# Attention output evacuated per two head pairs, and PSUM banks handed out in the order of their release

## The chip, the core and the metric

The kernel runs on one core of one Trainium2 chip. The metric is device time in microseconds of one execution, and the time before is the median of three runs. The engines are called as in the profile: PE is TensorE (matmuls; PEld is its loading of weights), ACT is ScalarE, DVE is VectorE, POOL is GpSimd, and SP issues nearly all of the DMAs. The granted clock of TensorE is given as a share of its full speed.

## What is computed

A trunk of two layers over 256 tokens of width 1024. Each layer is a SwiGLU feed-forward, a token mixer, and a second feed-forward, all with RMS norms before and after and with residual sums. The mixer of the first layer is a gated linear recurrence; that of the second is a causal attention with 16 heads of width 64 and a forget bias, whose keys and values come from the stream after the first layer. All weights are float32 and are read from HBM. The change touches the attention:

```python
def forgetting_attention(xq, w_q, w_o, k, v, c):
    Bn, S, _ = xq.shape
    q = (xq @ w_q).reshape(Bn, S, N_HEADS, HEAD_DIM).transpose(0, 2, 1, 3) * (HEAD_DIM ** -0.5)
    outs = []
    for blk in range(S // Q_BLOCK):
        q0 = blk * Q_BLOCK
        end = q0 + Q_BLOCK
        logits = jnp.einsum('bhqd,bhkd->bhqk', q[:, :, q0:end], k[:, :, :end]).astype(jnp.float32)
        logits = logits + c[:, :, q0:end, None] - c[:, :, None, :end]
        ...
        p = jax.nn.softmax(logits, axis=-1).astype(v.dtype)
        outs.append(jnp.einsum('bhqk,bhkd->bhqd', p, v[:, :, :end]))
    o = jnp.concatenate(outs, axis=2).transpose(0, 2, 1, 3).reshape(Bn, S, D_ATTN)
    return o @ w_o
```

## The kernel before

**Tiling.** The 256 tokens are two tiles of 128, t = 0 and t = 1. Every float32 product is made of three: a weight is split into an upper half `whi` (ACT, L200) and a lower half `wlo` (DVE, L201), and so are the activations; `mm3` (L208 to L210) multiplies x-upper by whi, x-upper by wlo, and x-lower by whi into one PSUM bank. Weights arrive in 512 KB pieces; there are nine buffers for split weights, so a split of a later piece waits until TensorE has done with the piece that held its buffer.

**Banks.** PSUM is one tile `pall` of eight banks. `bank(kind)` hands them out from three lists: "mm" (0 to 3, for accumulators and small transposes), "gt" (4, 5) and "tr" (6, 7). It takes the first bank of the list that is neither held nor lent, and puts it at the list's end; with `hold` the bank stays taken until `release`. With `again` it takes the last free one of the list in place of the first. `release` only ends the hold, so the list is in the order of handing out. The waits that guard a bank are made by the framework from who reads and writes it.

**Attention.** `attention(t)` makes a list of steps. A step holds up to three pieces for different score groups: `values(i - 3)`, `turn(i - 2)` and `logits(i)`. A group is two head pairs for t = 0 (four groups) and one pair for t = 1 (eight groups).
- `logits` multiplies queries with keys (L1155) into two of the banks 4 to 7; DVE adds the bias (L1162) and takes the maximum (L1164), ACT makes the exponentials `pe` (L1170), DVE the reciprocal of their sum (L1172) and the product (L1173).
- `turn` transposes `pe` on TensorE (L1179) into an "mm" bank, taken with `again`; ACT copies it to `pT` (L1181).
- `values` multiplies `pT` with the values (L1193) into the held "mm" bank `po`. A bank holds four head pairs. When it is full, ACT copies it to `oh` (L1199), DVE subtracts to get `ol` (L1200), and the bank is released.

The queries are made by the projection before it (`heads_T`, whose ACT copy to `qT` is L1025), and the output projection (`row_items`, `mm3` on `oh` and `ol`) takes one head pair k = 0 to 7 as a row; the last two rows of a tile are kept and done together. `enter` then norms the sum and adds it to `h` (L315, L319).

**Order.** TensorE's order is written by hand. In the attention it is the string `ATT_ORDER`: "0" and "1" are the next unit of the query or output projection for that token tile, "a0" and "a1" the next step of the attention of that tile. So the projection rows of t = 0 run between the attention steps of t = 1. The framework's scheduler sets the order on ACT and DVE, which work in order, each instruction waiting for its inputs, its buffer and its bank.

Of the kernel before, what the change touches and what calls it, by code (L numbers as in the profile page):

```python
# [9 lines left out]
F32 = mybir.dt.float32  # L10
F32R = mybir.dt.float32r
BF16 = mybir.dt.bfloat16
AF = mybir.ActivationFunctionType
ALU = mybir.AluOpType
AX = mybir.AxisListType

P = 128
D = 1024
S = 256
# [26 lines left out]
def trunk_kernel(ctx: ExitStack, tc: tile.TileContext, A: dict, out: bass.AP):  # L46
    nc = tc.nc
# [11 lines left out]
    def nm(s):  # L59
        uid[0] += 1  # L60
        return f"{s}_{uid[0]}"

    pall = psum.tile([P, 8, 512], F32, name="pall")
    lent = set()
    order = {"mm": [0, 1, 2, 3], "gt": [4, 5], "tr": [6, 7]}
    held = {}

    def bank(kind, hold=False, again=False):

        free = [i for i in order[kind] if i not in held and i not in lent]  # L70
        i = free[-1 if again else 0]
        order[kind].remove(i)
        order[kind].append(i)
        b = pall[:, i, :]
        if hold:
            held[i] = b
        return b

    def release(*banks):
        for b in banks:  # L80
            for i in [i for i, v in held.items() if v is b]:
                del held[i]

    def mmbank():
        return bank("mm", True)

    def gtbank():
        return bank("gt")

    def trbank(hold=False):  # L90
        return bank("tr", hold)
# [326 lines left out]
    def proj_items(w, c0, nn, get_x, post, nk=8):  # L418

        kper = min(1024 // nn, 4)  # L420
        acc = {}

        for k0 in range(0, nk, kper):
            kn = min(kper, nk - k0)

            def prep(k0=k0, kn=kn):
                return split(load_raw(w[k0 * P:(k0 + kn) * P, c0:c0 + nn].rearrange("(k p) n -> p k n", p=P), P, kn * nn),
                             P, kn * nn)

            def work(t, u, k0=k0, kn=kn):  # L430
                if k0 == 0:
                    acc[t] = mmbank()
                ps = acc[t][:, :nn]
                for j in range(kn):
                    k = k0 + j
                    mm3(ps, *get_x(t, k), u.hi[:, j * nn:(j + 1) * nn], u.lo[:, j * nn:(j + 1) * nn], k == 0, k == nk - 1)
                if k0 + kn == nk:
                    post(t, acc[t][:, :nn])
                    release(acc[t])
            items.append((prep, work))  # L440
# [23 lines left out]
    def row_items(w, widths, get_x, post, rows=2):  # L464


        acc = {}
        kept = [[], []]
        nk = len(widths)
        r0 = 0  # L470
        for k, kp in enumerate(widths):
            def prep(kp=kp, r0=r0):
                return split(load_raw(w[r0:r0 + kp, :], kp, D), kp, D)

            def work(t, u, k=k):
                if k == 0:
                    acc[t] = [mmbank(), mmbank()]
                m = rows if t == 1 else min(rows, 2)
                if k >= nk - m:
                    kept[t].append((k, u))  # L480
                    if k < nk - 1:
                        return
                    todo = [(kk, uu, n) for n in range(2) for (kk, uu) in kept[t]]
                else:
                    todo = [(k, u, n) for n in range(2)]
                for (kk, uu, n) in todo:
                    mm3(acc[t][n], *get_x(t, kk), uu.hi[:, n * 512:(n + 1) * 512], uu.lo[:, n * 512:(n + 1) * 512],
                        kk == 0, kk == nk - 1)
                if k == nk - 1:
                    post(t, acc[t])  # L490
                    release(*acc[t])
            items.append((prep, work))
            r0 += kp
# [624 lines left out]
    att = {}  # L1118
# [17 lines left out]
    def attention(t):  # L1136

        ap = pools["a"]
        nk = t + 1
        per = 4 // nk  # L1140
        np_ = per // 2
        w = nk * P
        box = {}
        G = NH // per

        def head(hg, b, j):
            return 2 * (hg * np_ + j) + b

        def logits(hg):
            c = 4 + (hg % 2) * 2  # L1150
            lg = pall[:, c:c + 2, :S]
            for j in range(np_):
                for b in range(2):
                    p = hg * np_ + j
                    nc.tensor.matmul(lg[:, b, j * w:(j + 1) * w], att["q"][t][b * HD:(b + 1) * HD, p, :],  # L1155
                                     kv["kT"][b * HD:(b + 1) * HD, p, :w], start=True, stop=True)
            v = lg.rearrange("p b (j k) -> p j b k", j=np_)
            h0 = hg * per
            bias = att["nb"][t][:, h0:h0 + per, :].rearrange("p (j b) k -> p j b k", b=2)
            if np_ == 1:  # L1160
                v, bias = lg, att["nb"][t][:, h0:h0 + per, :]
            nc.vector.tensor_tensor(v, v, bias, ALU.add)  # L1162
            mx = spool.tile([P, 4], F32, tag="mx", name=nm("mx"))[:, :per]
            nc.vector.tensor_reduce(mx, lg.rearrange("p b (j k) -> p b j k", j=np_), AX.X, ALU.max, negate=True)  # L1164
            sm = spool.tile([P, 4], F32, tag="sm", name=nm("sm"))[:, :per]
            pe = box["pe", hg] = ap.tile([P, per, w], F32, tag="pe", name=nm("pe"), bufs=2)
            for b in range(2):
                for j in range(np_):
                    i = b * np_ + j
                    nc.scalar.activation(pe[:, i, :], lg[:, b, j * w:(j + 1) * w], AF.Exp, bias=mx[:, i:i + 1],  # L1170
                                         accum_out=sm[:, i:i + 1])
            nc.vector.reciprocal(sm, sm)  # L1172
            nc.vector.tensor_tensor(pe, pe, sm.unsqueeze(2).to_broadcast([P, per, w]), ALU.mult)  # L1173

        def turn(hg):
            tp = bank("mm", again=True)
            pev = box["pe", hg].rearrange("p a b -> p (a b)")
            for j in range(4):
                nc.tensor.transpose(tp[:, j * P:(j + 1) * P], pev[:, j * P:(j + 1) * P], ident)  # L1179
            pT = box["pT", hg] = ap.tile([P, 4, P], F32, tag="pT", name=nm("pT"), bufs=2)  # L1180
            nc.scalar.activation(pT.rearrange("p a b -> p (a b)"), tp, AF.Copy)  # L1181

        def values(hg):
            p0 = hg * np_
            if p0 % 4 == 0:
                box["po"] = mmbank()
            po, pT = box["po"], box["pT", hg]
            for j in range(np_):
                o = (p0 + j) % 4 * P
                for k in range(nk):  # L1190
                    for b in range(2):
                        hd = head(hg, b, j)
                        nc.tensor.matmul(po[b * HD:(b + 1) * HD, o:o + P], kv["v"][k][:, hd * HD:(hd + 1) * HD],  # L1193
                                         pT[:, (b * np_ + j) * nk + k, :], start=k == 0, stop=k == nk - 1)
            if (p0 + np_) % 4 == 0:
                b = (p0 + np_) // 4 - 1
                oh_v = att["oh"][t][:, 4 * b:4 * b + 4, :].rearrange("p a b -> p (a b)")
                ol_v = att["ol"][t][:, 4 * b:4 * b + 4, :].rearrange("p a b -> p (a b)")
                nc.scalar.activation(oh_v, po, AF.Copy)  # L1199
                nc.vector.tensor_tensor(ol_v, po, oh_v.bitcast(F32), ALU.subtract)  # L1200
                release(po)

        steps = []
        for i in range(G + 3):
            s = []
            if 0 <= i - 3 < G:
                s.append(lambda i=i: values(i - 3))
            if 0 <= i - 2 < G:
                s.append(lambda i=i: turn(i - 2))
            if i < G:  # L1210
                s.append(lambda i=i: logits(i))
            steps.append(s)
        return steps
# [13 lines left out]
    ffn_d = ffn_items(lambda: pools["f"], A["ffn2_w_gate"][1], A["ffn2_w_up"][1], A["ffn2_w_down"][1], A["ffn2_post_g"][1],  # L1227
                      lambda t, hid: None, last=True)

    ATT_ORDER = ("0 0 0 0 0 0 0 a0 0 a0 1 1 1 a0 1 1 a0 1 1 a0 1 a1 0 a0 0 a1 0 a0 0 a1 0 a1 0 a1 0 a1 0 a1 1 a1 1 a1 1 a1 1 a1 1 1 1 1")  # L1230


    def half(t, i):
# [139 lines left out]
    nxt = [n_ffn3, n_ffn3]  # L1373
    for c in ATT_ORDER.split():
        if c[0] == "a":
# [45 lines left out]
```

## Time and profile before

| | us |
|---|---|
| median of three runs (lowest, highest) | 1004.15 (1004.14, 1004.41) |
| the profiled execution | 1002.69 |
| its span, from first to last instruction | 1001.0 |
| mean granted clock of TensorE | 0.997 |
| attention and output projection, from the span's start | about 738 to 812 |

The profile is of one execution. A row of the timeline has the start and the length in us, the engine, the line of the kernel, the operation, what it writes and reads, how many instructions were merged, and in brackets the engine's idle time before it with what ended that. A row of a stretch has its length, each engine's busy time with its number of instructions, the granted clock, the DMA share and GB/s. Where a line was used for several shapes, a group's mean mixes them.

### The profile page before, as it was taken

To read this page: it belongs to the slowest core of one execution; us is meant where nothing else is said; L and a number is where in the kernel's file an instruction comes from. 1 tells how busy PE (TensorE), PEld (TensorE's weight loads), DVE (VectorE), ACT (ScalarE), POOL (GpSimd) and SP (SyncE) were. 2 spreads that over 40 slices of the span, in tenths; PEclk is the share of its full clock that TensorE was granted. 3 is DMA by queue.
4 is the path that set the end of the run, shared out by engine and by line. 5 is a ranking of instruction groups with operands and counts; after the bars stand their busy time and mean duration, and the time that the engine had idled before them with its cause. 6 is when DMAs were issued, how large, how long until landed. Compare 5 with 4: busy or idle time off the path is not lost.

```text
span 1001.0 us, 13884 instructions
## 1 busy us (share of the span) xinstructions
PE 983.4 (98%) x5292; PEld 836.0 (84%) x5292; DVE 677.0 (68%) x787; ACT 563.5 (56%) x736; POOL 52.1 (5%) x97
## 2 busy tenths in 40 slices
PE   8999999999999999999999999999999999999997
PEld 6888888889978888888898888888876678888886
DVE  5977664668997766664697666764587757666542
ACT  6666544559986655543565555543466656555431
POOL 3300000100003000000100000000030000000000
PEclk9999999999999999999999999999999999999999
DMA  7887645565336766546368666655485158665431
GB/s 237 262 274 232 200 160 189 166 180 154 110 105 225 237 185 191 190 164 173 118 220 270 175 193 192 189 180 168 151 291 169 43 148 251 188 192 189 152 123 42
DMA packets 94632, 182.06 MB, mean 182 GB/s; under 512 B 11854, under 2 KB 34470, under 8 KB 94438
## 3 DMA queue, kind: packets, MB, share of 16 engines
q1 hardware_dynamic: 93894, 181.10, 58.2%
q8 instruction: 41, 0.67, 0.3%
q0 software_dynamic: 640, 0.07, 0.1%
q14 instruction: 25, 0.20, 0.1%
q10 hardware_dynamic: 32, 0.01, 0.0%
HBM read 180.09 MB, written 1.06 MB: 181 GB/s over the span
## 4 chain that ended last, share of the span: by engine, by line
PE 68%; issue 22%; ACT 5%; DVE 3%; POOL 1%; DMA 0%; SPq 0%; DVEq 0%; POOLq 0%; ACTq 0%
PE pall L234 24%; PE pall L236 12%; PE pall L208 9%; PE pall L210 9%; PE pall L209 8%; PE pall L851 1%; PE pall L215 1%; PE pall L216 1%; PE pall L217 1%; ACT junk L249 1%; ACT whi L200 1%; DVE wlo L201 1%; POOL rstd L244 1%; DVE h L319 1%; POOL nv L242 0%
## 5 line engine op out<-in xcount | busy, mean ns | idle before, releaser
L201 DVE TENSOR_TENSOR wlo<-raw,whi 128x1024 fp32r<-128x1024 f32 (+4 forms) x329 | 394.5, 1206 | 246.5 <-ACT whi L200 245.5
L200 ACT ACTIVATE whi<-raw 128x1024 fp32r<-128x1024 f32 (+4 forms) x329 | 341.3, 1044 | 289.8 <-PE pall L210 115.5
L234 PE MATMUL pall<-xall,whi 128*128 128x512 f32 x1280 | 349.1, 394 | 1.5 <-DVE xall L1275 1.5
L234 PEld LDWEIGHTS pall<-xall,whi 128*128 128x128 f32 x1280 | 218.8, 188 | 30.9 <-DVE xall L1275 2.4
L236 PEld LDWEIGHTS pall<-xall,wlo 128*128 128x128 f32 x1280 | 195.8, 188 | 28.4 <-DVE wlo L201 0.5
L236 PE MATMUL pall<-xall,wlo 128*128 128x256 f32 x1280 | 203.7, 281 | 0.1
L208 PE MATMUL pall<-whi,hid 128*128 128x512 f32 (+2 forms) x400 | 153.1, 383 | 0.5 <-ACT v L1102 0.5
L210 PE MATMUL pall<-whi,hid 128*128 128x512 f32 (+2 forms) x400 | 152.4, 381 | 0.0
L209 PE MATMUL pall<-wlo,hid 128*128 128x512 f32 (+2 forms) x400 | 152.4, 381 | 0.0
L208 PEld LDWEIGHTS pall<-whi,hid 128*128 128x128 f32 x400 | 75.1, 188 | 14.5 <-ACT v L1102 0.8
L210 PEld LDWEIGHTS pall<-whi,hid 128*128 128x128 f32 x400 | 75.1, 188 | 13.9
L209 PEld LDWEIGHTS pall<-wlo,hid 128*128 128x128 f32 x400 | 75.1, 188 | 13.3
L242 POOL TENSOR_SCALAR nv<-ss 128x1 f32<-128x1 f32 x24 | 10.3, 429 | 937.1 <-ACT junk L249 937.0
L208 PE MATMUL pall<-whi,xall 128*128 128x512 f32 (+2 forms) x144 | 57.4, 398 | 0.3 <-DVE t L315 0.3
L210 PE MATMUL pall<-whi,xall 128*128 128x512 f32 (+2 forms) x144 | 55.2, 383 | 0.0
L209 PE MATMUL pall<-wlo,xall 128*128 128x512 f32 (+2 forms) x144 | 55.0, 382 | 0.0
L587 ACT ACTIVATE sil<-sil 128x1024 f32<-128x1024 f32 (+1 forms) x22 | 21.7, 984 | 25.8 <-DVE sil L586 25.8
L597 ACT ACTIVATE hid<-prod 128x1024 fp32r<-128x1024 f32 (+1 forms) x22 | 21.6, 984 | 19.8 <-DVE prod L593 19.8
L208 PEld LDWEIGHTS pall<-whi,xall 128*128 128x128 f32 x144 | 27.1, 188 | 5.6 <-DVE t L315 0.7
L210 PEld LDWEIGHTS pall<-whi,xall 128*128 128x128 f32 x144 | 27.0, 188 | 5.4 <-DVE xall L272 0.3
L209 PEld LDWEIGHTS pall<-wlo,xall 128*128 128x128 f32 x144 | 27.1, 189 | 4.5
L313 DVE SCALAR_TENSOR_TENSOR t<-pall,rstd,gb 128x512 f32<-128x512 f32 x16 | 11.9, 748 | 26.7 <-ACT junk L249 26.7
(193 smaller groups left out, 981.2 us busy)
## 6 DMA issues: line engine op xcount, KB each, us to landing
raw<-in_ffn_w_down_dram SPq DMA_DIRECT2D x88, 512.0 KB
raw<-in_ffn_w_up_dram SPq DMA_DIRECT2D x80, 512.0 KB
raw<-in_ffn_w_gate_dram SPq DMA_DIRECT2D x78, 512.0 KB
raw<-in_rg_w_in_dram SPq DMA_DIRECT2D x20, 504.0 KB
raw<-in_ffn_w_gate_dram SPq DMA_DIRECT2D x20, 256.0 KB
raw<-in_rg_w_out_dram SPq DMA_DIRECT2D x10, 504.0 KB
raw<-in_ffn_w_up_dram SPq DMA_DIRECT2D x16, 256.0 KB
raw<-in_w_kv_dram SPq DMA_DIRECT2D x8, 512.0 KB
```

The source lines that it names most:

```text
L200: nc.scalar.activation(hi[:parts, c:c + m], rawv[:, c:c + m], AF.Copy)
L201: nc.vector.tensor_tensor(lo[:parts, c:c + m], rawv[:, c:c + m], hi[:parts, c:c + m].bitcast(F32), ALU.subtract)
L208: nc.tensor.matmul(ps, xh, wh, start=first, stop=False)
L209: nc.tensor.matmul(ps, xh, wl, start=False, stop=False)
L210: nc.tensor.matmul(ps, xl, wh, start=False, stop=last)
L215: nc.tensor.matmul(ps, wh, xh, start=first, stop=False)
L234: nc.tensor.matmul(o[:, b], w, both, start=k == 0, stop=False)
L236: nc.tensor.matmul(oh[:, b], w, upper, start=False, stop=k == 7)
L242: nc.gpsimd.tensor_scalar(v, ss[:, 0:1], ss[:, 1:2] if n == 2 else 0.0, D * EPS * f * f, ALU.add, ALU.add)
L313: nc.vector.scalar_tensor_tensor(t1[n], pf[n], r_in, gb[:, n * 512:(n + 1) * 512], ALU.mult, ALU.mult)
L587: nc.scalar.activation(s, s, AF.Silu)
L597: nc.scalar.activation(hv, pv, AF.Copy)
```

## The change

`values` now evacuates after two head pairs in place of four, so `oh` and `ol` are written in eight pieces of 128x256 in place of four of 128x512, and `po` is held for half as long and is half used. `release` moves the released bank to the end of its list, so that the list is in the order in which banks were released or handed out without a hold, whichever came last. `turn` loses `again` and takes the first free bank. The string `ATT_ORDER` is only written on two lines.

```diff
-    def bank(kind, hold=False, again=False):
-
-        free = [i for i in order[kind] if i not in held and i not in lent]
-        i = free[-1 if again else 0]
+    def bank(kind, hold=False):
+
+        i = [i for i in order[kind] if i not in held and i not in lent][0]
         order[kind].remove(i)
         order[kind].append(i)
...
         for b in banks:
             for i in [i for i, v in held.items() if v is b]:
                 del held[i]
+                kind = [n for n in order if i in order[n]][0]
+                order[kind].remove(i)
+                order[kind].append(i)
...
-            tp = bank("mm", again=True)
+            tp = bank("mm")
...
-            if p0 % 4 == 0:
+            if p0 % 2 == 0:
                 box["po"] = mmbank()
             po, pT = box["po"], box["pT", hg]
             for j in range(np_):
-                o = (p0 + j) % 4 * P
+                o = (p0 + j) % 2 * P
...
-            if (p0 + np_) % 4 == 0:
-                b = (p0 + np_) // 4 - 1
-                oh_v = att["oh"][t][:, 4 * b:4 * b + 4, :].rearrange("p a b -> p (a b)")
-                ol_v = att["ol"][t][:, 4 * b:4 * b + 4, :].rearrange("p a b -> p (a b)")
-                nc.scalar.activation(oh_v, po, AF.Copy)
-                nc.vector.tensor_tensor(ol_v, po, oh_v.bitcast(F32), ALU.subtract)
+            if (p0 + np_) % 2 == 0:
+                k0 = p0 + np_ - 2
+                oh_v = att["oh"][t][:, k0:k0 + 2, :].rearrange("p a b -> p (a b)")
+                ol_v = att["ol"][t][:, k0:k0 + 2, :].rearrange("p a b -> p (a b)")
+                nc.scalar.activation(oh_v, po[:, :S], AF.Copy)
+                nc.vector.tensor_tensor(ol_v, po[:, :S], oh_v.bitcast(F32), ALU.subtract)
                 release(po)
```

TensorE's instructions and SP's DMAs stand in the same order as before. What moves is the order on ACT and DVE in the attention, and the bank that each user gets. Lines after the first hunk are two or three higher in the changed kernel: L1199 becomes L1201, L1200 becomes L1202.

On ACT, where the query projection of t = 1 ends and the exponentials of score group 3 of t = 0 (`pe_6719` before, `pe_6721` now) are due; before:

```order
L200 ACTIVATE whi_6739<-raw_6737 128x1024
L1025 ACTIVATE qT_6489<-pall 128x512
L200 ACTIVATE whi_6751<-raw_6749 128x1024
L1170 ACTIVATE pe_6719,sm_6718<-pall,mx_6716 128x128 x4
L1199 ACTIVATE oh_6491<-pall 128x512
L1181 ACTIVATE pT_6765<-pall 128x512
L200 ACTIVATE whi_6777<-raw_6775 128x1024
```

and now:

```order
L202 ACTIVATE whi_6741<-raw_6739 128x1024
L1027 ACTIVATE qT_6489<-pall 128x512
L202 ACTIVATE whi_6753<-raw_6751 128x1024
L1201 ACTIVATE oh_6491<-pall 128x256
L1183 ACTIVATE pT_6767<-pall 128x512
L202 ACTIVATE whi_6779<-raw_6777 128x1024
L1172 ACTIVATE pe_6721,sm_6720<-pall,mx_6718 128x128 x4
```

The four exponentials moved from ahead of the copy to `oh`, the copy to `pT` and the next weight split (`whi_6777`, now `whi_6779`) to behind all three.

On DVE at the same place, from the lower half of the piece before to the product of group 3; before:

```order
L201 TENSOR_TENSOR wlo_6752<-raw_6749,whi_6751 128x1024
L1172 RECIPROCAL sm_6718<-sm_6718 128x4
L1019 TENSOR_SCALAR htok_6773<-pall,rstd_6534 128x512
L1173 TENSOR_TENSOR pe_6719<-pe_6719,sm_6718 128x512
L1200 TENSOR_TENSOR ol_6493<-pall,oh_6491 128x512
L201 TENSOR_TENSOR wlo_6778<-raw_6775,whi_6777 128x1024
L1162 TENSOR_TENSOR pall<-pall,nb_6483 128x2x256
```

and now:

```order
L203 TENSOR_TENSOR wlo_6754<-raw_6751,whi_6753 128x1024
L1202 TENSOR_TENSOR ol_6493<-pall,oh_6491 128x256
L1021 TENSOR_SCALAR htok_6775<-pall,rstd_6534 128x512
L203 TENSOR_TENSOR wlo_6780<-raw_6777,whi_6779 128x1024
L1174 RECIPROCAL sm_6720<-sm_6720 128x4
L1164 TENSOR_TENSOR pall<-pall,nb_6483 128x2x256
L1175 TENSOR_TENSOR pe_6721<-pe_6721,sm_6720 128x512
```

The reciprocal and the product of group 3 moved behind the lower half of the next weight and, the product, behind the bias add for the first group of t = 1.

On DVE in the attention of t = 1, the pieces of `ol` for that tile are `ol_6494`; the first of the four stands like this now:

```order
L1166 TENSOR_REDUCE mx_6888<-pall 128x2
L1174 RECIPROCAL sm_6890<-sm_6890 128x2
L1175 TENSOR_TENSOR pe_6891<-pe_6891,sm_6890 128x512
L1202 TENSOR_TENSOR ol_6494<-pall,oh_6492 128x256
L1164 TENSOR_TENSOR pall<-pall,nb_6483 128x2x256
```

and the second:

```order
L317 TENSOR_TENSOR t_1094_6965<-pall,gb_6634 128x512
L321 SCALAR_TENSOR_TENSOR h<-t_1093_6963,rstd_6969,h 128x512
L321 SCALAR_TENSOR_TENSOR h<-t_1094_6965,rstd_6969,h 128x512
L1202 TENSOR_TENSOR ol_6494<-pall,oh_6492 128x256
L1164 TENSOR_TENSOR pall<-pall,nb_6483 128x2x256
```

The second of them stands where the first whole `ol` of that tile stood, behind the two updates of `h`; the first has no counterpart before.

More of the change, by code (lines that the diff above doesn't have):

```diff
@@ L1228, in trunk_kernel @@
                       lambda t, hid: None, last=True)
-    ATT_ORDER = ("0 0 0 0 0 0 0 a0 0 a0 1 1 1 a0 1 1 a0 1 1 a0 1 a1 0 a0 0 a1 0 a0 0 a1 0 a1 0 a1 0 a1 0 a1 1 a1 1 a1 1 a1 1 a1 1 1 1 1")
+    ATT_ORDER = ("0 0 0 0 0 0 0 a0 0 a0 1 1 1 a0 1 1 a0 1 1 a0 1 a1 0 a0 0 a1 0 a0 0 a1 0 a1 0 a1 0 a1 0 a1 "
+                 "1 a1 1 a1 1 a1 1 a1 1 1 1 1")
     def half(t, i):
```

## Prediction

> **What bounds the kernel now.** I read the page's busy shares first, then the stage that the change touches as one stretch, then TensorE's timeline in it. In the stretch rows the columns are: length, busy time of an engine (and its instructions), then the granted clock and the DMA share.
>
> ```profile
> PE 983.4 (98%) x5292; PEld 836.0 (84%) x5292; DVE 677.0 (68%) x787; ACT 563.5 (56%) x736; POOL 52.1 (5%) x97
> ...
> L201 DVE TENSOR_TENSOR wlo<-raw,whi 128x1024 fp32r<-128x1024 f32 (+4 forms) x329 | 394.5, 1206 | 246.5 <-ACT whi L200 245.5
> ...
> 738.00:812.00 74.00, 69.15 (x408) 48.70 (x407) 55.21 (x83) 46.87 (x114) 8.11 (x9) 0.98 0.43 143
> 812.00:830.00 18.00, 18.00 (x89) 15.06 (x88) 10.04 (x13) 10.28 (x14) 1.02 (x3) 1.00 0.52 158
> ```
>
> TensorE is busy 98% of the span, so time is won or lost only where it waits or where its clock falls. Attention and the output projection lie in 738 to 812 us: there TensorE is idle for 74.00 - 69.15 = 4.85 us and its clock is 0.98; in the feed-forward behind it, it is never idle. Its timeline shows nearly all of that as seven waits (in brackets: idle time, and what ended it).
>
> ```profile
> 748.48 0.40 PE L210 MATMUL pall<-whi,xall 128*128 128x512 f32 x1
> 749.20 0.66 PE L1179 MATMUL pall<-ident,pe 128*128 128x128 f32 x4 [0.32 <-ACT qT L1025]
> ...
> 758.62 0.66 PE L1193 MATMUL pall<-pT,v 128*64 128x128 f32 x8
> ...
> 761.19 0.70 PE L1155 MATMUL pall<-kT,qT 64*128 64x256 f32 x4
> 762.20 0.47 PE L208 MATMUL pall<-whi,oh 128*128 128x512 f32 x1 [0.30 <-ACT pT L1181]
> 762.50 0.40 PE L209 MATMUL pall<-wlo,oh 128*128 128x512 f32 x1
> 763.31 0.50 PE L210 MATMUL pall<-whi,ol 128*128 128x512 f32 x1 [0.40 <-DVE ol L1200]
> 763.64 0.40 PE L208 MATMUL pall<-whi,oh 128*128 128x512 f32 x1
> ...
> 765.02 0.66 PE L1179 MATMUL pall<-ident,pe 128*128 128x128 f32 x4
> ...
> 777.88 0.66 PE L1193 MATMUL pall<-pT,v 128*64 128x128 f32 x8
> ...
> 779.87 0.66 PE L1193 MATMUL pall<-pT,v 128*64 128x128 f32 x8
> ...
> 784.64 0.66 PE L1193 MATMUL pall<-pT,v 128*64 128x128 f32 x8
> ...
> 786.45 0.50 PE L208 MATMUL pall<-whi,oh 128*128 128x512 f32 x1
> 786.78 0.40 PE L209 MATMUL pall<-wlo,oh 128*128 128x512 f32 x1
> 788.88 0.50 PE L210 MATMUL pall<-whi,ol 128*128 128x512 f32 x1 [1.70 <-DVE ol L1200]
> ...
> 790.21 1.12 PE L1193 MATMUL pall<-pT,v 128*64 128x128 f32 x8
> ...
> 793.31 0.50 PE L208 MATMUL pall<-whi,oh 128*128 128x512 f32 x1
> ...
> 802.60 0.50 PE L208 MATMUL pall<-whi,oh 128*128 128x512 f32 x1 [1.04 <-ACT oh L1199]
> ...
> 804.01 0.50 PE L210 MATMUL pall<-whi,ol 128*128 128x512 f32 x1 [0.67 <-DVE ol L1200]
> ...
> 809.58 0.50 PE L208 MATMUL pall<-whi,xall 128*128 128x512 f32 x1 [0.29 <-DVE t L315]
> 809.92 0.40 PE L209 MATMUL pall<-wlo,xall 128*128 128x512 f32 x1
> 810.15 0.39 PE L210 MATMUL pall<-whi,xall 128*128 128x512 f32 x1
> ```
>
> Five of the seven are rows of the output projection, which wait for oh and ol of head pairs that are evacuated late, since a bank is emptied once per four pairs. The longest one, 1.70 us, is followed by half clock:
>
> ```profile
> 790.00:791.00 1.00, 1.00 (x9) 0.50 0.00 0
> ...
> 793.00:794.00 1.00, 1.00 (x7) 0.95 0.36 27
> ...
> 804.00:805.00 1.00, 0.99 (x4) 1.00 0.66 111
> ```
>
> The waits at 802.60 and 804.01 (1.04 and 0.67 us) are not followed by it.
>
> **What goes.** The idle times sum to 0.32 + 0.30 + 0.40 + 1.70 + 1.04 + 0.67 + 0.29 = 4.72 us. That is a lower bound of what they cost: after a wide matmul the next would have started 0.23 us behind it (809.92 to 810.15), not at the end of its 0.40 us, and the first matmul after a wait is followed 0.33 us later (763.31 to 763.64). So each of the four waits behind a wide matmul costs 0.17 + 0.10 us more, and I give the other three 0.1 us: 4.72 + 1.08 + 0.30 = 6.1 us. The half clock costs 3.10 us (790.21 to 793.31) against 1.81 us for the same three groups at full clock (784.64 to 786.45): 1.3 us. Why each goes:
> - 749.20: the turn took the bank used last, which the copy to qT still held; it now takes the one free the longest.
> - 762.20, 763.31, 788.88, 802.60, 804.01: a projection row needs only its own pair. Pairs 0 and 1 are now emptied two pairs earlier than pairs 2 and 3, so rows 0 and 4 find their operands; the last rows need pairs 6 and 7 only at the very end, some twelve wide matmuls (2.8 us at 0.23) after the last values.
> - 809.58: the next feed-forward's first bank was one that L315 was reading; it is now another.
>
> All of it, 6.1 + 1.3 = 7.4 us, lies on TensorE.
>
> **What comes.** Four evacuations on either engine become eight of half the width. No 128x256 evacuation to oh or ol is in the trace; ACT's nearest row is the 128x256 copy from PSUM at L298, and VectorE's the 253-wide tap from PSUM at L809 (second row of this fence).
>
> ```profile
> L298 ACT ACTIVATE rrow<-pall 128x256 f32<-128x256 f32 x2 | 0.8, 384 | 3.6 <-PE pall L296 3.6
> ...
> 256.68 0.47 DVE L809 SCALAR_TENSOR_TENSOR xc<-pall,par,xc 126x253 f32<-126x253 f32 x1
> ...
> 257.38 0.36 PE L215 MATMUL pall<-xall,whi 128*126 128x256 f32 x1
> ...
> 758.73 1.06 ACT L200 ACTIVATE whi<-raw 128x1024 fp32r<-128x1024 f32 x1 [0.29 <-PE pall L210]
> 759.70 0.35 ACT L1170 ACTIVATE pe<-pall,mx 128x128 f32<-128x128 f32 x1
> ...
> 757.37 0.68 DVE L1173 TENSOR_TENSOR pe<-pe,sm 128x512 f32<-128x512 f32 x1
> ...
> 761.22 0.18 DVE L1172 RECIPROCAL sm<-sm 128x4 f32<-128x4 f32 x1 [0.17 <-ACT pe L1170]
> ...
> 779.23 0.69 DVE L1173 TENSOR_TENSOR pe<-pe,sm 128x512 f32<-128x512 f32 x1
> 779.84 0.69 DVE L1162 TENSOR_TENSOR pall<-pall,nb 128x512 f32<-128x512 f32 x1
> ...
> 786.81 1.41 DVE L319 SCALAR_TENSOR_TENSOR h<-t,rstd,h 128x512 f32<-128x512 f32 x2 [0.25 <-POOL rstd L244]
> 788.14 0.68 DVE L1200 TENSOR_TENSOR ol<-pall,oh 128x512 fp32r<-128x512 f32 x1
> ```
>
> So a half costs about 0.38 us on ACT and 0.45 on VectorE (bounds: nothing, and a whole 0.68). Eight halves instead of four wholes are under 1 us more on engines that are busy 47 and 55 of these 74 us: nothing by itself. What costs is where TensorE waits anew.
>
> First, the turn of score group 3 (765.02). On ACT a weight split now stands ahead of that group's exponentials; it can start only once TensorE has left the rows that use its buffer, in the logits' slot of 761.19. From there: the split starts 0.11 us after the group behind such rows (758.62 to 758.73), 0.97 us to the exponentials (758.73 to 759.70), 1.52 us to the reciprocal (759.70 to 761.22), then 0.1 us, the next tile's bias add that now stands ahead (0.6 us, 779.23 to 779.84, is VectorE's step for such an operation), and the product itself (0.68): 4.0 us. TensorE needs 765.02 - 761.19 = 3.83 us for the way there, less the two waits that go (with their extra about 1.05): 2.8 us. New wait: 1.2 us. Behind it stand the next projection rows. Bounds: nothing, if the scheduler's order hides it, and 2.4 us, if one of VectorE's splits (1.2 us each, the L201 row) comes between.
>
> Second, the values of pair 2 of token tile 1 (779.87) reuse the bank that pairs 0 and 1 have just left, at 777.88 plus 0.66 us; of the group's other banks two are held and the third is the turn's. VectorE's product of 779.23 stands ahead of ol: 779.84 + 0.45 = 780.3 us, so 0.45 us of wait; taken as 0.6, since ACT's half and the next turn's copy share that interval. Third, the values at 790.21 reuse it again: ol, behind the same two h updates, ends about 788.14 + 0.45 = 788.6 us in old time. TensorE, freed of 1.70 us, gets there after six wide matmuls, at 786.45 + 6 x 0.23 + 0.2 = 788.05: 0.6 us of wait. So the longest old wait does not vanish; two thirds of it do. Bounds of these two: nothing, and 1.3 us each (one more VectorE split ahead).
>
> Sum of the new waits: 1.2 + 0.6 + 0.6 and 0.1 for each restart, 2.7 us; between 0 and 5.3.
>
> The new order of banks also moves accumulators in the earlier stages. The one place that comes near a wait is the recurrent stage: a projection at 257.38 now gets a bank whose last reader ends at 256.68 + 0.47 = 257.15. The bank counts as released where the release was written down, not where VectorE was done; 0.23 us of slack is left, so I take nothing (bound: 1 us, were VectorE one split later).
>
> Net: 7.4 - 2.7 = 4.7 us. The profiled execution took 1002.69 us (span 1001.0 and 1.7 around it) and would take 998.0; the timed median is 1.46 us higher for reasons the trace does not show, so the forecast is 1004.15 - 4.7 = 999.5 us. The part's own range, from the bounds: 4.72 + 1.3 - 5.3 = 0.7 us gained at least, 7.4 at most: 996.8 to 1003.4.
>
> [...] The clock fell after 1.70 us of idle here. [...]
>
> **The rivals.**
> - Half clock after a new wait. The trace has it after 1.70 us of idle and not after 1.04; the new 1.2 us wait lies between. It would cost the same 1.3 us: 1000.8. For it: the projection goes straight on behind it. Against: 1.2 is nearer to 1.04. Chance 0.12.
> - The half clock has another cause than the wait and stays, whatever the wait becomes: 1.3 us of the sum fall away, 1000.8. For it: 1.04 and 0.67 us of idle within 2.5 us had no effect. Against: it begins right behind the longest wait of the whole trace. [...]
> - The gain is given back: the feed-forward behind 812 us could be held by its weights and end when it did, 1004.2. Against: TensorE is busy for all of the 18 us behind 812, and the DMA share there is 0.52. Also here: the new waits near their upper bounds eat the gain. Chance 0.10.
> - Slower. All second pairs of a tile now go through one bank, emptied by in-order ACT and VectorE. If a lower-half split (1.2 us) stands ahead of ol at each of the three reuses of tile 1 (3.6 us) and two of the longer waits halve the clock (2.6), the net is 4.7 - 6.2 = -1.5: 1005.7 us. It decides from 7.4 us of new cost. For it: VectorE's new order has a split ahead of one of the three, and the scheduler moved operations that I priced by old rows. Against: at that reuse TensorE arrives late enough, and the other two have a product or the h updates ahead, which I counted. Chance 0.13.
>
> **How the numbers follow.** Forecast 0.60. Measurements of this kernel tell a change from none at about 0.2%, 2.0 us. Faster by more than that: 0.60 + 0.12 + 0.05 = 0.77; within: 0.10; slower: 0.13. The time is that of the forecast, 999.5; the range goes from 997.5 (new waits near half of mine) up into the given-back case, 1004.0, and leaves out the slower one and the most lucky bounds.
>
> **What would show it.** In the new trace: no wait for qT at the first turn, none for oh or ol at the projection's rows, no half clock near 790; new waits of about 1.2, 0.6 and 0.6 us at the turn of group 3 and at two values groups, the latter two ended by ol. The recurrent stage and the feed-forwards take what they took. The prediction is wrong if the values wait for over 1.5 us anywhere, if the clock falls elsewhere, or if 738 to 812 is shorter by 4 to 5 us and the end is not.

## The result, and the profile after

| | before | changed |
|---|---|---|
| median, us (lowest to highest, runs) | 1003.70 (1001.15 to 1004.41, 6) | 997.88 (997.67 to 999.25, 6) |
| ratio, 95% interval | | 0.9948, 0.9936 to 0.996 |
| the profiled execution, us | 1002.69 | 999.25 |
| its span, us | 1001.0 | 997.5 |
| mean granted clock | 0.997 | 0.999 |

The changed kernel is faster by half a per cent: 5.8 us between the medians, 3.4 between the two profiled executions. The forecast was 999.5 us, 4.7 less than before. The page of the changed kernel has the same work on TensorE, and the stretches of the stage show where it goes (columns as in the prediction):

```profile
PE 982.6 (99%) x5292; PEld 837.2 (84%) x5292; DVE 676.6 (68%) x791; ACT 564.2 (57%) x740; POOL 52.5 (5%) x97
```

```profile
738.00:812.00 74.00, 71.23 (x433) 52.48 (x432) 59.19 (x92) 49.36 (x122) 9.61 (x12) 1.00 0.49 163
812.00:830.00 18.00, 18.00 (x85) 14.97 (x84) 10.53 (x13) 11.97 (x14) 0.80 (x2) 1.00 0.50 146
...
790.00:791.00 1.00, 0.59 (x8) 0.45 (x9) 0.96 (x3) 0.95 (x1) 0.00 (x0) 1.00 0.00 0
```

TensorE is idle for 74.00 - 71.23 = 2.77 us there, against 4.85, and the clock is 1.00 throughout. Its timeline in the stage:

```profile
749.92 0.39 PE L212 MATMUL pall<-whi,xall 128*128 128x512 f32 x1
750.15 0.60 PE L1181 MATMUL pall<-ident,pe 128*128 128x128 f32 x4
...
766.24 0.63 PE L1181 MATMUL pall<-ident,pe 128*128 128x128 f32 x4 [1.26 <-DVE pe L1175]
...
781.58 0.66 PE L1195 MATMUL pall<-pT,v 128*64 128x128 f32 x8 [0.64 <-DVE ol L1202]
...
788.70 0.40 PE L212 MATMUL pall<-whi,ol 128*128 128x512 f32 x1
...
790.41 0.66 PE L1195 MATMUL pall<-pT,v 128*64 128x128 f32 x8 [0.62 <-DVE ol L1202]
...
794.72 0.66 PE L1181 MATMUL pall<-ident,pe 128*128 128x128 f32 x4 [0.25 <-DVE pe L1175]
...
800.71 0.50 PE L210 MATMUL pall<-whi,oh 128*128 128x512 f32 x1
...
801.28 0.39 PE L212 MATMUL pall<-whi,ol 128*128 128x512 f32 x1
...
806.51 0.39 PE L211 MATMUL pall<-wlo,xall 128*128 128x512 f32 x1
```

No projection row waits any more (788.70, 800.71 and 801.28 carry no bracket), the first turn at 750.15 doesn't wait for qT, and four waits are new. I measure the stage from the projection's matmul at 748.48 us to the feed-forward's at 809.92 (both rows in the prediction): 61.44 us before. The same two matmuls stand at 749.92 and 806.51 now: 56.59 us, **4.85 us less**. From there to the last matmul, every kernel of this study takes the same 184.3 us.

The other 1.4 us of the difference went at the start of the profiled execution, where the change does nothing. The first projection rows of before and of the changed kernel, from their timelines:

```profile
6.01 1.20 PE L234 MATMUL pall<-xall,whi 128*128 128x512 f32 x4 [0.65 <-DVE xall L1275]
```

```profile
6.17 2.07 PE L236 MATMUL pall<-xall,whi 128*128 128x512 f32 x4 [0.23 <-DVE xall L1278]
```

The same four matmuls take 2.07 us in place of 1.20: the clock is not full yet. It rose to full at 4.62 us in the one execution and at 9.97 in the other, by the trace's record of the clock (the stretch rows of a profile show 1.00 there all the same). At 740 us the changed kernel is 1.44 us behind, and it was 1.43 behind at 20 us; 4.85 - 1.44 = 3.4 us is the difference of the spans.

### The profile page after: what moved, and what is told of

Its sections match the earlier page's. It is cut to its first block, busy times and chain, and to the rows that moved or that the text cites. A ratio compares the mean times of both kernels' runs of the same rounds, so it can differ in the third digit from the quotient of the medians.

```text
span 997.5 us, 13896 instructions
## 1 busy us (share of the span) xinstructions
PE 982.6 (99%) x5292; PEld 837.2 (84%) x5292; DVE 676.6 (68%) x791; ACT 564.2 (57%) x740; POOL 52.5 (5%) x97
## 4 chain that ended last, share of the span: by engine, by line
PE 68%; issue 21%; ACT 4%; DVE 3%; POOL 1%; DMA 1%; SPq 0%; DVEq 0%; POOLq 0%; ACTq 0%
PE pall L236 24%; PE pall L238 12%; PE pall L210 9%; PE pall L212 9%; PE pall L211 9%; PE pall L853 1%; PE pall L217 1%; PE pall L218 1%; PE pall L219 1%; ACT junk L251 1%; ACT whi L202 1%; DVE wlo L203 1%; POOL rstd L246 1%; DMA raw<-in_ffn_w_up_dram 1%; DVE h L321 1%
```

## The experiments

All kernels in one table. "Idle" is TensorE's idle time in 738 to 812 us, "stage" the time between the two matmuls named above, both in the profiled execution; a median stands beside that of the kernel before on the same chip.

| kernel | pairs per evacuation | turn's bank | release moves the bank | priority for oh, ol | idle, us | stage, us | median, us (before) |
|---|---|---|---|---|---|---|---|
| before | 4 | last | no | no | 4.85 | 61.44 | |
| changed | 2 | first | yes | no | 2.77 | 56.59 | 997.88 (1003.70) |
| before_again | 4 | last | no | no | 4.83 | 59.92 | one run: 1001.57 |
| before_filled | 4 | last | no | no | 3.92 | 59.93 | 1002.07 (1003.79) |
| split_only | 2 | last | no | no | 9.53 | 66.18 | 1007.46 (1002.93) |
| split_no_again | 2 | first | no | no | 6.23 | 62.53 | 1005.23 (1003.79) |
| banks_only | 4 | first | yes | no | 3.53 | 59.50 | 1000.65 (1002.93) |
| priority_only | 4 | last | no | yes | 3.67 | 58.65 | 1000.30 (1002.72) |
| banks_and_priority | 4 | first | yes | yes | 2.31 | 56.73 | 998.93 (1002.72) |
| changed_again | 2 | first | yes | no | 2.79 | 56.63 | 999.12 (1002.93) |
| evac_first_t0 | 2 | first | yes | tile 0 | 1.51 | 55.30 | 997.45 (1003.79) |
| evac_first | 2 | first | yes | yes | 0.75 | 54.54 | 996.88 (1002.93) |

### The halves of the change

**split_only** is the kernel before with the hunk in `values` alone:

```diff
-            if p0 % 4 == 0:
+            if p0 % 2 == 0:
...
-                nc.scalar.activation(oh_v, po, AF.Copy)
-                nc.vector.tensor_tensor(ol_v, po, oh_v.bitcast(F32), ALU.subtract)
+                nc.scalar.activation(oh_v, po[:, :S], AF.Copy)
+                nc.vector.tensor_tensor(ol_v, po[:, :S], oh_v.bitcast(F32), ALU.subtract)
```

> Only the evacuation per two pairs; banks as before (handed out in the order of handing out, the turn takes the last one). Theory (both parts are needed): with an evacuation in nearly every step, the bank handed out last is the one the values have just filled, so about six turns wait for their own step's oh and ol (0.38 and 0.45 us, and what stands ahead of them on ACT and VectorE, 0.5 to 3.5 us each, some 10 us in all), against 7.4 us that go with the late rows; some of these waits are above 1.7 us and halve the clock. Slower than before by 2 to 8 us, 1009 us. Rival (the split alone carries the gain, the bank rule only tidies): the waits of the late projection rows and the half clock go and nothing comes, 997 to 999 us.

It is slower, ratio 1.0048 (1.0035 to 1.0062), 4.5 us. The rival, that the split carries the gain, falls. TensorE's timeline, and VectorE's at the same place:

```profile
754.61 0.66 PE L1193 MATMUL pall<-pT,v 128*64 128x128 f32 x8
758.28 0.65 PE L1179 MATMUL pall<-ident,pe 128*128 128x128 f32 x4 [3.02 <-DVE ol L1200]
...
762.93 0.66 PE L1193 MATMUL pall<-pT,v 128*64 128x128 f32 x8
766.92 1.11 PE L1179 MATMUL pall<-ident,pe 128*128 128x128 f32 x4 [3.33 <-DVE ol L1200]
```

```profile
755.48 2.35 DVE L201 TENSOR_TENSOR wlo<-raw,whi 128x1024 fp32r<-128x1024 f32 x2
...
757.83 0.39 DVE L1200 TENSOR_TENSOR ol<-pall,oh 128x256 fp32r<-128x256 f32 x1
...
764.17 2.36 DVE L201 TENSOR_TENSOR wlo<-raw,whi 128x1024 fp32r<-128x1024 f32 x2 [0.53 <-ACT whi L200]
766.44 0.42 DVE L1200 TENSOR_TENSOR ol<-pall,oh 128x256 fp32r<-128x256 f32 x1
```

The values fill a bank, and the turn right behind them takes that same bank, the last handed out: it waits until ol, itself behind two weight splits, has emptied it. I expected six such turns and some 10 us; there are four, 7.5 us together.

**split_no_again** takes away the turn's special rule too, and leaves `release` as it was:

```diff
-            tp = bank("mm", again=True)
+            tp = bank("mm")
```

> The evacuation per two pairs, and the turn takes the first free bank; a release leaves the order as it is. Theory: the turn's two waits of 3.08 and 3.40 us, which came because the bank handed out last was the one the values had just filled, are gone or below 1 us; but without the move at release a held bank's place in the list is as old as its handing out, so it still comes too early for someone: two to three waits of 1 to 2.3 us remain. 1002 to 1006 us, between the changed kernel and the split alone. Rival (only the turn's last-bank rule stood in the way, the move at release adds nothing): as the changed kernel, within 0.7 us of it, 998 to 1000 us.

1005.23 us against 1003.79, ratio 1.0011 (0.9998 to 1.0024): no gain. The two 3 us waits are gone, but others have come, among them these:

```profile
755.55 0.66 PE L1193 MATMUL pall<-pT,v 128*64 128x128 f32 x8 [0.98 <-DVE htok L1019]
...
781.75 0.81 PE L1179 MATMUL pall<-ident,pe 128*128 128x128 f32 x4 [1.77 <-DVE ol L1200]
...
793.22 0.50 PE L208 MATMUL pall<-whi,oh 128*128 128x512 f32 x1 [1.03 <-DVE ol L1200]
...
800.32 0.66 PE L1179 MATMUL pall<-ident,pe 128*128 128x128 f32 x4 [2.15 <-DVE ol L1200]
```

A bank that was held stands in the list where its handing out put it, so it counts as long free the moment it is released. The move at `release` is what the split needs.

**banks_only** has the hunks in `bank`, `release` and `turn`, and the evacuation per four pairs.

> Only the rule of the banks; evacuation per four pairs as before. Theory: the turn's wait for qT (0.32) and the feed-forward's wait for L315 (0.29) go, with their extras about 0.8 us in all; the waits for ol and oh at the second and last quarter (1.70, 1.04, 0.67) and the half clock behind the longest stay, since the rows still wait for a whole bank. 738 to 812 us keeps over 3 us of TensorE's idle time; 1002.5 to 1003.5 us beside a before of 1003.7. Rival (the bank rule carries the gain): 738 to 812 keeps under 1.5 us of idle time, 999 us.

Faster, ratio 0.9974 (0.9965 to 0.9983), by 2.3 us. In the profiled execution the three longest waits and the half clock stay, as expected:

```profile
787.87 0.50 PE L212 MATMUL pall<-whi,ol 128*128 128x512 f32 x1 [1.70 <-DVE ol L1202]
...
801.60 0.50 PE L210 MATMUL pall<-whi,oh 128*128 128x512 f32 x1 [1.04 <-ACT oh L1201]
...
803.01 0.50 PE L212 MATMUL pall<-whi,ol 128*128 128x512 f32 x1 [0.68 <-DVE ol L1202]
```

But the gain is more than twice the 0.8 us that I gave it: 61.44 - 59.50 = 1.94 us of stage, with a half clock in both. The two waits that stood at 762.20 and 763.31 are gone as well, without the split. The first was ended by the copy to pT, which was emptying the very bank that the projection's row was given: a matter of banks, not of late pairs. The second goes because VectorE's order changed; before, and with the new rule of the banks:

```profile
761.31 0.74 DVE L1019 TENSOR_SCALAR htok<-pall,rstd 128x512 f32<-128x512 f32 x1
761.97 0.68 DVE L1173 TENSOR_TENSOR pe<-pe,sm 128x512 f32<-128x512 f32 x1
762.57 0.68 DVE L1200 TENSOR_TENSOR ol<-pall,oh 128x512 fp32r<-128x512 f32 x1
```

```profile
761.55 0.69 DVE L1202 TENSOR_TENSOR ol<-pall,oh 128x512 fp32r<-128x512 f32 x1 [0.31 <-ACT oh L1201]
762.16 0.68 DVE L1175 TENSOR_TENSOR pe<-pe,sm 128x512 f32<-128x512 f32 x1
762.76 0.74 DVE L1021 TENSOR_SCALAR htok<-pall,rstd 128x512 f32<-128x512 f32 x1
```

ol now stands first of the three and is done about 1 us earlier (762.24 against 763.25). And the turn of group 3 does not wait in this kernel: that new wait belongs to the split.

### The new waits

**evac_first** is the changed kernel with the evacuation put ahead:

```diff
-                nc.scalar.activation(oh_v, po[:, :S], AF.Copy)
-                nc.vector.tensor_tensor(ol_v, po[:, :S], oh_v.bitcast(F32), ALU.subtract)
+                with tc.high_priority():
+                    nc.scalar.activation(oh_v, po[:, :S], AF.Copy)
+                    nc.vector.tensor_tensor(ol_v, po[:, :S], oh_v.bitcast(F32), ALU.subtract)
```

> The changed kernel, and the scheduler is told to put the copy to oh and the subtraction to ol ahead of what is ready beside them. Theory: the waits left after the change (1.33 at 765.02, 0.53 at 779.87, 0.48 at 790.21, 0.32 at 795.50, 2.7 us in all) come from what stands ahead of oh, ol and the product of group 3 on ACT and VectorE; most of it goes, 1.5 to 2.2 us less than the changed kernel on the same chip, 996 us. Rival (the engines have no room: the exponentials or the splits that now stand behind come late in their turn): within 0.5 us of the changed kernel, with new waits elsewhere in 738 to 812.

996.88 us, ratio to before 0.9941 (0.9928 to 0.9955), and 2.2 us below the changed kernel on the same chip (2.1 in the stage): the fastest version here. TensorE's waits in 735 to 825 us (line, what it waited for, sum in us, times, longest):

```profile
PE pall L1195 <- ACT pT L1183: 0.4, 2, 0.2
PE pall L1181 <- DVE pe L1175: 0.4, 1, 0.4
```

The engines have the room (VectorE is busy for 60.97 and ACT for 51.16 of the 74 us); what was wrong was the order. On ACT the exponentials of group 3 start at 760.75 us and the weight split behind them at 762.13; in the changed kernel (changed_again's trace) the split came first, at 762.29, and the exponentials at 763.25:

```profile
760.75 0.37 ACT L1172 ACTIVATE pe<-pall,mx 128x128 f32<-128x128 f32 x1
...
762.13 1.08 ACT L202 ACTIVATE whi<-raw 128x1024 fp32r<-128x1024 f32 x1
```

```profile
762.29 1.06 ACT L202 ACTIVATE whi<-raw 128x1024 fp32r<-128x1024 f32 x1 [0.75 <-PE pall L212]
763.25 0.35 ACT L1172 ACTIVATE pe<-pall,mx 128x128 f32<-128x128 f32 x1
```

**evac_first_t0** does it for token tile 0 alone.

```diff
+                urgent = tc.high_priority() if t == 0 else ExitStack()
+                with urgent:
...
```

> The changed kernel, with oh and ol put ahead on ACT and VectorE for token tile 0 alone. Theory: the wait of 1.33 us at the turn of score group 3 (765.02 in the kernel before) goes, the waits of 0.5, 0.5 and 0.3 us at 779.87, 790.21 and 795.50, which belong to tile 1, stay; 1.2 us less than the changed kernel, 997.8 us beside 999.1. Rival (the wait at group 3 comes from something else than the place of the exponentials and the product): it stays, and the time is that of the changed kernel.

997.45 us; the stage is 55.30 us, 1.3 less than that of the changed kernel (56.59 and 56.63). The wait at group 3 is gone, those of tile 1 are there as before. So that one wait is worth 1.3 us and comes from the place of the exponentials and the product.

**priority_only** and **banks_and_priority** give the priority to whole 128x512 pieces, in the kernel before and in banks_only.

> The kernel before, with only the scheduler told to put oh and ol ahead (whole 128x512 pieces, banks as before). Theory: the wait of 1.70 us at 788.88 shrinks by the two updates of h that stood ahead of ol (1.41 us) to about 0.3, and the half clock there with it; the waits for qT, L315 and at 802.60 and 804.01 stay, since there the rows still wait for a whole bank. About 3.2 us of idle time in 738 to 812 (before 4.85), 1.5 to 3 us less than before in the median. Rival (the priority alone brings what evac_first brought): idle time under 1 us, 997 us.

> The rule of the banks and the priority of oh and ol, without the split: four pairs per evacuation. Theory (the split is worth the waits of the last rows of tile 1, 1.04 and 0.67 us, and the clock that they cost in some executions): about 2.2 us of idle time in 738 to 812 remain, most of it at 802.60 and 804.01 and at one turn (795.50, 0.4); 999 to 1000 us, 2 to 3 us above evac_first. Rival (the split is worth nothing once the order is right): within 0.7 us of evac_first, 996.2 to 997.6 us.

1000.30 us, ratio 0.997 (0.9956 to 0.9985), and 998.93, ratio 0.9953 (0.9935 to 0.9971). The wait of 1.70 us is gone from both traces (0.3 was expected to stay in the first), and so is the half clock. Idle time was expected at 3.2 and 2.2 us and is 3.67 and 2.31: in priority_only a projection row waits 0.8 us for a bank that htok is reading, which I had not foreseen. In banks_and_priority these waits remain:

```profile
PE pall L210 <- ACT oh L1202: 1.0, 1, 1.0
PE pall L212 <- DVE ol L1203: 0.6, 1, 0.6
PE pall L1181 <- DVE pe L1175: 0.3, 1, 0.3
PE pall L1195 <- ACT pT L1183: 0.2, 1, 0.2
```

The first two are those of the last quarter, where a row waits for the whole bank. The split takes them away: 56.73 - 54.54 = 2.2 us of stage from banks_and_priority to evac_first. On the other side banks_and_priority, without the split, is as fast as the change: the change pays for the split with new waits about what it wins by it.

### The clock

> The kernel before, unaltered, for a second trace. [...] The span is about 1000.7 without the half clock and 1002 with it. Rival (each wait of 1.70 us halves the clock): half clock near 790 again, whatever the rise.

> The changed kernel unaltered, for a second trace. Theory: the stage of the attention repeats (waits of 1.3 and 0.6 us at the turn of group 3 and at the values, no half clock), and what differs is only where the clock rises at the start: the first profile of it rose at 9.97 us and lost 1.4 us to that, a rise near 4.6 us as in the profile of before would give a span of 996.1. Rival (the 1.4 us at the start are the change's own): the rise is near 10 us again.

Both kernels unaltered. In before_again the wait is there, and no half clock behind it; its timeline and its stretches:

```profile
789.25 0.50 PE L210 MATMUL pall<-whi,ol 128*128 128x512 f32 x1 [1.69 <-DVE ol L1200]
```

```profile
790.00:791.00 1.00, 1.00 (x11) 0.47 (x10) 0.53 (x1) 0.52 (x1) 0.83 (x3) 1.00 0.00 0
```

The stage takes 59.92 us, 1.52 less than in the first execution of the same kernel. So the half clock is worth about 1.5 us and does not come each time; the span, 999.9, is the expected 1000.7 within a microsecond, and the rival falls. Why it came in the one execution and not in the other is not shown: the wait before it is 1.70 us there and 1.69 here.

changed_again repeats the stage (56.63 us, the same four waits). Its clock rose at 9.91 us again, so this run alone can't tell whether the late start is the change's own. evac_first, which holds the whole change, shows that it need not come: its clock rose at 5.58 us and it is 0.84 us behind at 740. Five of the six timed executions of the changed kernel also have spans of 996.0 to 996.5 us, 1.0 to 1.5 below the profiled 997.5. Whether the change makes a late start likelier is not shown: the rise came after 9.9 us in three of the four traces with the whole change, and in one of the eight others. Over the traces the rise lies anywhere from 4.62 to 10.71 us.

**before_filled** puts four wide matmuls into the wait; their result goes to a bank that nobody reads:

```diff
         nc.tensor.matmul(ps, xh, wl, start=False, stop=False)
+        if fill is not None:
+            for _ in range(4):
+                nc.tensor.matmul(fill, xh, wh, start=True, stop=True)
...
```

> The kernel before with four more wide matmuls (0.23 us each, their result in a bank that nobody reads) in the wait of 1.70 us at 788.88. The wait for ol stays as long, but TensorE works for 0.9 us of it. Theory (idle time halves the clock): the row's third matmul starts when it did, no half clock near 790 in the profiled execution or in the mean clocks of the timed ones, and the median is 0.4 to 1.3 us below that of before. Rival (the half clock has another cause): mean clocks of 0.995 to 0.997 in about half of the executions as before, median as before.

Its timeline at the place:

```profile
787.37 1.09 PE L212 MATMUL pall<-whi,oh 128*128 128x512 f32 x4
789.22 0.50 PE L213 MATMUL pall<-whi,ol 128*128 128x512 f32 x1 [0.77 <-DVE ol L1204]
```

Nothing is shortened, TensorE only works in the wait, and the kernel is faster: ratio 0.9985 (0.9975 to 0.9994), 1.7 us between the medians, a little more than the 0.4 to 1.3 expected. The stage is that of before_again, 59.93 against 59.92 us, both without the half clock. None of its ten executions has a mean clock of 0.995, against 7 of the 19 of the kernel before on the same chip; two have 0.997, so the half clock isn't gone from all of them; the waits at 802.60 and 804.01 were left as they are. This agrees with idle time as the cause and doesn't settle it: banks_only, whose three waits were not filled, also has eight of ten executions at 0.998 or 0.999. The 43 executions of the kernel before that were timed beside the experiments, grouped by their mean clock, fit the same reading:

| mean granted clock | executions | median, us |
|---|---|---|
| 0.998 or 0.999 | 16 | 1002.54 |
| 0.996 or 0.997 | 16 | 1003.69 |
| 0.995 | 11 | 1005.26 |

The groups lie 1.2 and 1.6 us apart, about one half clock each: none, one, or two. They are not clean, since the mean clock also holds the half clock behind the last matmuls (1.1 to 4.5 us of the span in the traces), and not the late start. The second half clock would be at 802.60 and 804.01, the only other long waits; that is argued from these numbers, since no profiled execution has it.

## Why the prediction was right, point by point

The forecast's net was 4.7 us and the stage gives 4.85, in an execution of before that had the half clock. By the starts of the same matmuls in both traces (the extra of the next matmul included):

| step | forecast, us | measured, us |
|---|---|---|
| waits removed, with extras | 6.1 | 0.55 + 0.34 + 0.68 + 1.97 + 1.12 + 0.94 + 0.57 = 6.17 |
| half clock | 1.3 | 1.30 from 790.21 on; 1.52 in all, between two executions of before |
| turn of group 3 | -1.2 | -1.30 |
| values at 779.87 | -0.6 | -0.53 |
| values at 790.21 | -0.6 | -0.48 |
| turn at 795.50 | not foreseen | -0.32 |
| restarts | -0.3 | contained in the above |
| recurrent stage, feed-forwards | 0 | 0 within 0.1 |

- **What goes:** each of the seven waits is gone, and their sum with the extras holds within 0.1 us. The reason given for two of them was wrong. 762.20 and 763.31 were put down to the split ("a projection row needs only its own pair"); banks_only removes both. 762.20 had "ACT pT" in its bracket, a copy that reads a bank and makes nothing that this row needs: that was to be read as a wait for a bank.
- **What comes:** the three places, what ends each wait, and the sizes were right. (The arrival at 790.21 was added up 0.02 us too late, 788.05 for 788.03; nothing hangs on it.) The evacuation's halves take 0.376 us on ACT and 0.412 on VectorE, against 0.38 and 0.45 from the nearest rows (changed kernel, groups of 738 to 812):

```profile
L1202 DVE TENSOR_TENSOR ol<-pall,oh 128x256 fp32r<-128x256 f32 x8 | 3.3, 412 | 0.0
L1201 ACT ACTIVATE oh<-pall 128x256 fp32r<-128x256 f32 x8 | 3.0, 376 | 0.4 <-PE pall L1195 0.4
```

  The wait at 795.50 was missed: there the product of one group ends a little too late for a turn that now comes sooner, since the rows ahead of it no longer wait. It is the size of the restarts, and so the sum stayed right by luck.
- **The half clock:** its size was right, its rule wrong. The prediction read one execution and took the length of the wait to decide, "after 1.70 us of idle and not after 1.04". It counts in some executions and not in others, and the shorter pair of waits seems to cost it too in some. Read as none, one and two, the groups of the 43 executions give (16 + 2 x 11) / 43 = 0.9 half clocks to each, an estimated 1.3 us by the mean: the term's size stands, for another reason. Where the execution of before has no half clock, the stage gains 59.92 - 56.63 = 3.29 us (before_again, changed_again).
- **The median:** the measured difference is 5.8 us in one comparison and 3.8 in the other (changed_again, ratio 0.9963, 0.995 to 0.9977). The medians of before differ by 0.8 us there and those of the changed kernel by 1.2: which executions lose the clock, and when it rises at the start, can move a median by more than most of the terms. The three runs shown, 1004.15, lie above the 1003.22 of the 43 later ones, and the forecast carried over the 1.46 us by which they lay above the profiled execution. The changed kernel has no such surplus: its median, 997.88, lies 1.4 us below its profiled execution, near the 998.0 that the sum gave before it was added. That 999.5 agrees with the profiled 999.25 is luck, since that execution had the late start.
- **The rivals:** the 1.26 us wait did not halve the clock in the two profiles. The gain wasn't given back: the feed-forward is never idle in 812 to 830. That the half clock had another cause than idle time (0.05 of the forecast's chances) is unlikely: in the twelve traces it came four times before 985 us, each time right behind a wait, of 1.70 us in before and in banks_only, 3.33 in split_only and 1.77 in split_no_again; before_filled agrees. The slower case named the right weakness, VectorE's and ACT's order at the reuse of a bank; split_only shows how far it goes, two splits ahead of ol and 3 us of wait, when the reuse comes at once.

## What to carry to other kernels

Emptying a bank in smaller pieces shortens the wait of those who need the data, but it makes banks change hands more often: here it paid only once the next user got the bank that had been free the longest, by release and not by handing out. After such a change look at what the scheduler puts ahead of the evacuations on the in-order engines; giving them priority was worth another 2.1 us of the stage here. Compare stages between two fixed instructions, not whole times: executions of the kernel before alone lay between 1001.2 and 1005.8 us, and in the traces such differences come from the start and the clock.

## What the runs showed of the hardware

In the four traces with a half clock inside the kernel (before, banks_only, split_only, split_no_again) it lasts 3.4 us each time (3.413 in before, by the trace's record of the clock). The length of the wait ahead of it doesn't decide alone. split_only had a wait of 3.02 us that ended at 758.28 without a fall of the clock, and one of 3.33 us that ended at 766.92 with one; split_no_again fell after 1.77 us and not after 2.15. Their stretches behind these waits, split_only first:

```profile
759.00:760.00 1.00, 1.00 (x10) 0.83 (x11) 0.34 (x1) 0.57 (x1) 0.00 (x0) 1.00 1.06 391
...
767.00:768.00 1.00, 1.00 (x5) 1.00 (x6) 0.00 (x0) 0.00 (x0) 0.00 (x0) 0.50 0.75 285
```

```profile
783.00:784.00 1.00, 1.00 (x8) 0.36 (x6) 0.24 (x1) 0.19 (x1) 0.00 (x0) 0.50 0.00 0
...
801.00:802.00 1.00, 1.00 (x6) 0.78 (x6) 0.06 (x1) 0.60 (x1) 0.00 (x0) 1.00 0.77 141
```

The wait of 1.70 us was followed by a fall in before and in banks_only, that of 1.69 us in before_again was not, and neither were those of 1.04 and 0.67 us in the profiled execution of before. What decides besides the length is not shown.
